# Two-layer hybrid decoder on one core: the experts' low rows subtracted on VectorE instead of GpSimd, with a narrow-product estimate changed and the schedule's priorities drawn anew

## The chip, the cores and the metric

The kernel runs on one core of a Trainium2 chip. The metric is the device time of one execution in microseconds (us), lower is better; the number that counts is the median of three runs. The core's engines appear in the profile as PE (TensorE), DVE (VectorE), ACT (ScalarE), POOL (GpSimd) and SP (SyncE, which issues the transfers from HBM). PEclk is the granted clock of TensorE as a share of its full 2.4 GHz, so 0.50 is the level of 1.2 GHz.

## The reference

T = 256 rows of D = 1024 float32 numbers go through two layers. Each layer adds a mixer, an attention over a memory of its own, and a mixture of 16 experts, each behind an RMS norm:

```
for l in range(DEPTH):
    x = x + hybrid_mixer(rmsnorm(x, mix_norm_g[l]), ...)
    x = x + memory_cross_attention(rmsnorm(x, xattn_norm_g[l]), rmsnorm(mem, mem_norm_g[l]), wq, wkv, wo)
    x = x + hierarchical_moe(rmsnorm(x, ffn_norm_g[l]), wg, bg, we, be, w1, w3, w2)
return rmsnorm(x, final_norm_g)
```

The mixture picks, for each row, one of 4 groups by the largest of 4 logits and two of the group's 4 experts by the largest of their logits; the row then runs through those two experts only, silu(h w1) * (h w3), times w2, weighted.

## The kernel before

**Numbers in two parts.** Products are made at float32 accuracy from TensorE's faster fp32r format. A float32 tensor is rounded to a high part (a copy or activation, mostly on ACT), and the low part is the difference: `split` and `wsplit` put the high part on ACT and the subtraction on DVE. A product is then three matmuls, high by high, high by low and low by high. In the names of the rows `w` is a 1 MB weight buffer, `wh` and `wl` its parts in slices of 512, `mTh` and `mTl` the parts of the memory rows, `yh` and `yl` those of an attention output, `x` the 256 x 1024 stream of rows itself in four blocks of 128 x 512, `ps` a PSUM bank.

**The order.** Nothing runs where it is written. Every call is recorded (line 120 issues them all, so that each row of the profile says L120) and a list scheduler, `Plan.order`, plays the recorded operations through with an estimate of each one's time (`Plan.cost`). On each engine it takes, of what could start now, the operation with the lowest priority number: its place in the program plus a bias for its step and one for its step and engine, from the table `BIAS`. On PE an operation may also be taken that could start up to `LOOK` ns later than the earliest if it has the same form (rows and columns of the array in use, 128 x 128 or a narrower tile), and one of another form is set back by `STICK`. The order that comes out is fixed: every engine runs its list in that order, and waits at an instruction whose inputs are not there.

**The stage around the change.** At the end of the cross attention (steps `wo0` to `wo3`) the blocks of `x` are finished by four adds on DVE (`x<-ps,xsu,x`). Then `route` (steps `r0` and `n0` in the first layer, `r1` and `n1` in the second):

- 16 transposes on PE bring `x` into four PSUM banks (`ps<-cst,x`), and four copies make `qT` of them, three on ACT and one, by `V.tensor_copy if n > b`, on DVE;
- 16 matmuls that fill a quarter of the array each (`ps<-qT,wg`, each two records in the trace) and two small ones (`ps<-cst,t`) give the router's 20 logits `lg`;
- some twenty short DVE operations rank them, down to `asg` and `pos`, and one-hot matrices `S` follow;
- the rows themselves are split for the experts: `nh` is the rounded `x`, two blocks by ACT and two by DVE, and `nl` = `x` - `nh` in four blocks, on GpSimd;
- the experts begin with `ga`, matmuls of `S` by `nh` and by `nl`, which pick each expert's rows (`ps<-S,nh`); then come `up` and `down` for two experts at a time, and `sc`, which puts the results back.

While the router's short chain runs, PE has other work. In layer 0 it is the second layer's memory keys, steps `mk0.1` and `mk1.1`: 48 matmuls of three kinds (`mTh,wh`, `mTl,wh`, `mTh,wl`) into each of two banks, whose `wl` DVE makes slice by slice. In layer 1 nothing is left over, and 24 matmuls whose result is not used (step `idle`, `ps<-nh`) take their place.

Of the kernel before, what the change touches and what calls it, by code (L numbers as in the profile page):

```python
# [13 lines left out]
ALU = mybir.AluOpType  # L14
# [30 lines left out]
HOLD = 0  # L45

DRAIN = 95
STICK = 200
LOOK = 40

LOAD = 0.82
# [72 lines left out]
class Plan:  # L124
# [24 lines left out]
    def cost(self, key, name, args, kw, outs, ins):  # L149
        def free(ap):  # L150
            n = 1
            for s, c in ap.ap[1:]:
                n *= c
            return n

        n = max(free(x) for x in outs[:1] + ins) if ins else free(outs[0])
        if key == "pe":
            w = free(outs[0])
            rhs = args[2] if len(args) > 2 else kw["rhs"]
            if name == "transpose":  # L160
                return max(w * 0.8333, 107) + 2
            if rhs.dtype == F32R:
                c = max(w * (0.4414 if w >= 256 else 1.0) + 5, 109)
            else:
                c = max(w * 1.6667 + 4, 218)
            return c
        psum = any(x.tensor.space == PS for x in ins)
        vec = sum(x.ap[0][1] == P and free(x) == 1 for x in ins[1:])
        if key == "act":
            return n * 0.8333 + (51 if psum else 93) + 93 * vec + 93 * ("accum_out" in kw)  # L170
        if key == "dve":
            if name == "reciprocal":
                return 68 + 6.4 * n
            two = name in ("tensor_tensor", "scalar_tensor_tensor", "tensor_tensor_scan", "tensor_reduce")
            if name == "tensor_tensor_scan":
                return 68 + n * 2.0834
            if not two and not psum:
                return 68 + n * 0.5208 + 61 * (vec > 0)
            return 68 + n * 1.0417 + 61 * (vec > 0)
        return 628 if name == "tensor_tensor" and n < 16 else 150 + 2.1 * n  # L180
# [11 lines left out]
    def note(self, keys, emit, name, args, kw):  # L192
# [24 lines left out]
        op.tiles = []  # L217
        op.prio = op.i + BIAS.get(self.step, 0) + BIAS.get(f"{self.step}/{keys[0]}", 0)
        op.eng, op.wait = keys[0], None
# [42 lines left out]
    def order(self, reserve):  # L262
# [59 lines left out]
        while left:  # L322
            best = None
            for e, cand in ready.items():
# [25 lines left out]
                for s, op in items:  # L350
                    if s <= s_min + (LOOK if e == "pe" and op.form == form else 0):
                        key = op.prio
                        if e == "act" and op.table and table not in op.table:
                            key += 60
                        if e == "pe" and op.form != form:
                            key += STICK
                        if pick is None or key < pick[0]:
# [70 lines left out]
def body(tc, nc, a):  # L428
    def fb(ap):
        return ap.bitcast(F32)  # L430

    with ExitStack() as es:
# [31 lines left out]
        def run(rounds, queue):  # L464
            plan = Plan(tc, nc, queue)
            TE, A, V, G, dq = (plan.queue(k) for k in ("pe", "act", "dve", "pool", "dma"))
# [6 lines left out]
            x = sp.tile([P, 2, D], F32, name="x")  # L473
# [8 lines left out]
            if rounds == 1:  # L482
# [5 lines left out]
                for i in range(4):  # L488
# [4 lines left out]
                    f = slice(i * 512, (i + 1) * 512)  # L493
# [694 lines left out]
            def route(l):  # L1188
# [27 lines left out]
                nh = tp.tile([P, 2, D], F32R, name="nh", tag="th")  # L1216
                nl = tp.tile([P, 2, D], F32R, name="nl", tag="tl")
                for n in range(2):
                    f = slice(n * 512, (n + 1) * 512)
                    for b in range(2):  # L1220
                        plan.step = f"n{l}"
                        (V.tensor_copy if n else A.copy)(nh[:, b, f], x[:, b, f])
                        G.tensor_tensor(nl[:, b, f], x[:, b, f], fb(nh[:, b, f]), op=ALU.subtract)
# [22 lines left out]
                for b in range(2):  # L1246
                    V.tensor_tensor(before[:, b], l5[:, b, :, None, :].to_broadcast([P, 5, 4, 4]), l5[:, b, :, :, None].to_broadcast([P, 5, 4, 4]),
                                    op=ALU.is_ge)
# [39 lines left out]
                w1 = sm.tile([P, 2, 4], F32, name="w1", bufs=1)  # L1288
# [12 lines left out]
                for b in range(2):  # L1301
                    w = pick[:, b * (P + 6 * NPAIR):b * (P + 6 * NPAIR) + 6 * NPAIR].rearrange("p (q c) -> p q c", c=6)
# [190 lines left out]
            for l in range(DEPTH):  # L1493
                mixers(l)
                plan.step = f"x{l}"
                attend(l)
                plan.step = ""
                nxt = l + 1 < DEPTH
                if nxt:
                    memory(l + 1)  # L1500
                plan.step = f"r{l}"
                routed = route(l)
                plan.step = ""
                if nxt:
                    fill(GAP)
                extras = [(kp, "bv"), (kp, "W1"), (kp, "W2"), (sp, "vm")]
                if not nxt:
                    extras += [(sp, "kT"), (sp, "mTh"), (sp, "mTl")]
                extras += [(kp, "qT"), (kp, "xn")] + ["t2"] * (NT2 // 4)
                for rnd in range(rounds):  # L1510
                    end = not nxt and rnd == rounds - 1
                    experts(l, rnd, extras, routed, ending if end else None, last_square if end else None)
# [109 lines left out]
```

## Time and profile before

| | |
|---|---|
| three runs | 731.29, 731.1, 730.45 us; median 731.1 |
| profiled execution | 731.96 us, of which the span from the first to the last instruction is 730.1 |
| busy | PE 712.4 us (98%), DVE 465.8, ACT 355.0, POOL 27.0 |
| mean granted PE clock | 0.992 |
| moved from HBM | 173.19 MB, 239 GB/s over the span |

A busy share says how long an engine had an instruction in flight, not how fast it was: a PE at half its clock is busy too. So the stretches are to be read with the clock beside the busy time, and the small idle time of PE with what released it.

### The profile page before, as it was taken

The numbers are of one execution on the slowest core, as the hardware profiler recorded it, in microseconds if no ns is written. First come the engines' busy times: TensorE is split into PE (matmuls) and PEld (weight loads), VectorE is DVE, ScalarE is ACT, GpSimd is POOL, SyncE is SP. The second block draws the span as 40 slices with busy tenths as digits, with TensorE's granted clock in tenths as the row PEclk, the third lists the DMA queues.
The fourth block names the chain that finished last, engine by engine and source line by source line (L and its number), as shares of the span: only waits on it lengthen the run. The fifth ranks groups of instructions, "written<-read, shape, count | busy, mean of one in ns | idle before, by whom it ended". The sixth has DMA issues, their size and how long they took to land.

```text
span 730.1 us, 12559 instructions
## 1 busy us (share of the span) xinstructions
PE 712.4 (98%) x4864; PEld 559.0 (77%) x4864; DVE 465.8 (64%) x1036; ACT 355.0 (49%) x724; POOL 27.0 (4%) x35
## 2 busy tenths in 40 slices
PE   8999999999999899999999999999999999999995
PEld 8988999989987863554469999888999874544552
DVE  6778699887699741233247669898867893322314
ACT  7666676657566311121146557885656542210212
POOL 0000000100001100000000000001000030000000
PEclk9999999999999899999999999999999999999998
DMA  8832444847645449999864543455577657899911
GB/s 319 334 124 108 140 181 162 308 168 267 213 162 196 174 169 427 401 391 425 331 240 168 181 172 137 145 198 206 174 264 266 234 202 298 350 417 423 386 71 62
DMA packets 30595, 175.13 MB, mean 240 GB/s; under 512 B 3520, under 2 KB 5696, under 8 KB 11072
## 3 DMA queue, kind: packets, MB, share of 16 engines
q1 hardware_dynamic: 30528, 174.25, 62.7%
q8 instruction: 40, 0.66, 0.3%
q14 instruction: 27, 0.22, 0.1%
HBM read 173.19 MB, written 1.05 MB: 239 GB/s over the span
## 4 chain that ended last, share of the span: by engine, by line
PE 88%; DVE 7%; ACT 3%; DMA 1%; issue 1%; SPq 0%; DVEq 0%; POOL 0%; ACTq 0%; POOLq 0%
PE ps L120 88%; DVE wl L120 1%; DVE S L120 1%; DVE OT L120 1%; DMA W<-in_mem 1%; ACT S L120 1%; DVE t L120 1%; DVE x L120 0%; ACT xn L120 0%; DVE nh L120 0%; SPq L120 0%; DVE qT L120 0%; DVE W L120 0%; ACT OT L120 0%; ACT wh L120 0%
## 5 line engine op out<-in xcount | busy, mean ns | idle before, releaser
L120 ACT ACTIVATE wh<-w 128x512 fp32r<-128x512 f32 (+1 forms) x256 | 159.2, 630 | 120.3 <-PE ps L120 110.9
L120 DVE TENSOR_TENSOR wl<-w,wh 128x512 fp32r<-128x512 f32 (+1 forms) x256 | 175.1, 697 | 53.6 <-ACT wh L120 50.3
L120 PE MATMUL ps<-tl,wh 128*128 128x256 f32 x448 | 126.6, 285 | 0.4 <-DVE tl L120 0.4
L120 PE MATMUL ps<-th,wh 128*128 128x256 f32 x448 | 126.4, 284 | 0.0
L120 PE MATMUL ps<-th,wl 128*128 128x256 f32 x448 | 125.6, 284 | 0.2 <-DVE wl L120 0.2
L120 PEld LDWEIGHTS ps<-tl,wh 128*128 128x128 f32 x448 | 84.1, 188 | 1.7 <-issue 1.0
L120 PEld LDWEIGHTS ps<-th,wl 128*128 128x128 f32 x448 | 83.8, 188 | 1.8 <-issue 0.9
L120 PEld LDWEIGHTS ps<-th,wh 128*128 128x128 f32 x448 | 84.2, 188 | 1.1 <-issue 0.5
L120 DVE TENSOR_TENSOR wl<-ps,wh 128x512 fp32r<-128x512 f32 x32 | 21.7, 690 | 65.2 <-ACT wh L120 59.7
L120 DVE SCALAR_TENSOR_TENSOR t<-t,ps 128x256 f32<-128x256 f32 (+1 forms) x20 | 9.5, 474 | 71.2 <-ACT t L120 71.2
L120 PE MATMUL ps<-wl,yh 128*128 128x512 f32 x128 | 50.5, 399 | 0.0
L120 PE MATMUL ps<-wh,yl 128*128 128x512 f32 x128 | 50.0, 397 | 0.0
L120 ACT ACTIVATE wh<-ps 128x512 fp32r<-128x512 f32 x32 | 18.8, 597 | 60.1 <-PE ps L120 60.1
L120 PE MATMUL ps<-wh,yh 128*128 128x512 f32 x128 | 46.2, 397 | 0.0
L120 ACT ACTIVATE t<-ps,cs 128x256 f32<-128x256 f32 x16 | 7.6, 475 | 75.3 <-PE ps L120 72.9
L120 PE MATMUL ps<-mTh,wl 128*128 128x256 f32 x128 | 37.9, 297 | 0.1
L120 PE MATMUL ps<-mTl,wh 128*128 128x256 f32 x128 | 37.2, 291 | 0.0
L120 PE MATMUL ps<-mTh,wh 128*128 128x256 f32 x128 | 37.2, 291 | 0.0
L120 PE MATMUL ps<-wl,mTh 128*128 128x256 f32 x128 | 36.7, 287 | 0.0
L120 PE MATMUL ps<-wh,mTl 128*128 128x256 f32 x128 | 36.2, 283 | 0.0
L120 PE MATMUL ps<-wh,mTh 128*128 128x256 f32 x128 | 36.0, 283 | 0.0
L120 PE MATMUL ps<-S,nh 128*128 128x256 f32 x128 | 32.3, 288 | 0.5 <-DVE pos L120 0.3
(308 smaller groups left out, 1618.7 us busy)
## 6 DMA issues: line engine op xcount, KB each, us to landing
w<-in_ws SPq DMA_DIRECT2D x97, 1024.0 KB, 4.9
W<-in_ws SPq DMA_DIRECT2D x15, 1024.0 KB, 8.2
bv<-in_ws SPq DMA_DIRECT2D x8, 1024.0 KB, 7.6
t<-in_ws SPq DMA_DIRECT2D x28, 256.0 KB, 6.7
vm<-in_ws SPq DMA_DIRECT2D x7, 1024.0 KB, 9.8
qT<-in_ws SPq DMA_DIRECT2D x7, 1024.0 KB, 9.5
xn<-in_ws SPq DMA_DIRECT2D x7, 1024.0 KB, 10.5
mTh<-in_ws SPq DMA_DIRECT2D x3, 1024.0 KB, 9.7
```

Of the source, the lines that this page charges most:

```text
L120: return self.plan.note([self.key], {self.key: lambda: getattr(self.real, name)(*args, **kw)}, name, args, kw)
```

## The change

Three edits. The low part of the experts' rows, `nl`, is subtracted on VectorE (`V.`) where GpSimd (`G.`) did it: eight instructions in all, four in each layer. In `Plan.cost` the estimate of an fp32r matmul loses its case for outputs narrower than 256 (which counted 1.0 ns a column) and its floor goes from 109 to 113 ns. The numbers that set the order, `BIAS`, `STICK` and `LOOK`, are other ones. What is computed, and the number of instructions of every kind, stay as they were.

```diff
-BIAS = {'xs0': 1235, 'cl0': -6235, 'gd0': -710, 'o30': -580, 'm0': 3495, 'w0': 7800,
...
+BIAS = {'xs0': 4070, 'cl0': -850, 'gd0': -450, 'o30': -355, 'm0': -1550, 'w0': 9125,
...
-STICK = 200
-LOOK = 40
+STICK = 300
+LOOK = 20
...
             if rhs.dtype == F32R:
-                c = max(w * (0.4414 if w >= 256 else 1.0) + 5, 109)
+                c = max(w * 0.4414 + 5, 113)
...
                         (V.tensor_copy if n else A.copy)(nh[:, b, f], x[:, b, f])
-                        G.tensor_tensor(nl[:, b, f], x[:, b, f], fb(nh[:, b, f]), op=ALU.subtract)
+                        V.tensor_tensor(nl[:, b, f], x[:, b, f], fb(nh[:, b, f]), op=ALU.subtract)
```

The places where the new order tells are these. On DVE in layer 0's `route`, before: from the last two adds of `x` to the copy `qT` (here `x_90` is the stream, `wl_675` and `wl_677` are slices of the memory key's weight).

```order
L120 SCALAR_TENSOR_TENSOR x_90<-ps_622,xsu_564,x_90 128x512
L120 SCALAR_TENSOR_TENSOR x_90<-ps_623,xsu_564,x_90 128x512
L120 CAST nh_647<-x_90 128x512 x2
L120 TENSOR_TENSOR wl_675<-w_670,wh_674 128x512
L120 TENSOR_TENSOR wl_677<-w_670,wh_676 128x512
L120 COPY qT_632<-ps_634 128x512
```

And the same place after, with the same names (`nl_648` was on POOL before; `w_680` is the next 1 MB of the memory key's weight):

```order
L120 SCALAR_TENSOR_TENSOR x_90<-ps_622,xsu_564,x_90 128x512
L120 SCALAR_TENSOR_TENSOR x_90<-ps_623,xsu_564,x_90 128x512
L120 TENSOR_TENSOR wl_677<-w_670,wh_676 128x512
L120 TENSOR_TENSOR wl_679<-w_670,wh_678 128x512
L120 TENSOR_TENSOR nl_648<-x_90,nh_647 128x512
L120 CAST nh_647<-x_90 128x512 x2
L120 TENSOR_TENSOR nl_648<-x_90,nh_647 128x512 x2
L120 TENSOR_TENSOR wl_683<-w_680,wh_682 128x512
L120 TENSOR_TENSOR wl_685<-w_680,wh_684 128x512
L120 COPY qT_632<-ps_634 128x512
```

Between the last add and `qT` stood two casts and two `wl`; now there are two casts, three `nl` and four `wl`.

On PE at the same place, before: from the last transposes (`ps_636`) over the router's matmuls (`ps_643`, `ps_645`), with the memory key's matmuls (`ps_671`) between.

```order
L120 MATMUL ps_636<-cst_82,x_90 128x128 x4
L120 MATMUL ps_643<-qT_632,wg_631 32x128 x4
L120 MATMUL ps_671<-mTh_625,wh_672 128x256
L120 MATMUL ps_671<-mTl_626,wh_672 128x256
L120 MATMUL ps_671<-mTh_625,wl_673 128x256
L120 MATMUL ps_671<-mTh_625,wh_672 128x256
L120 MATMUL ps_645<-qT_632,wg_631 32x128 x8
L120 MATMUL ps_671<-mTl_626,wh_672 128x256
L120 MATMUL ps_643<-qT_632,wg_631 32x128 x4
```

And after:

```order
L120 MATMUL ps_636<-cst_82,x_90 128x128
L120 MATMUL ps_671<-mTl_626,wh_678 128x256
L120 MATMUL ps_636<-cst_82,x_90 128x128
L120 MATMUL ps_671<-mTh_625,wl_679 128x256
L120 MATMUL ps_671<-mTh_625,wh_678 128x256
L120 MATMUL ps_671<-mTl_626,wh_678 128x256
L120 MATMUL ps_671<-mTh_625,wl_679 128x256
L120 MATMUL ps_643<-qT_632,wg_631 32x128 x4
L120 MATMUL ps_645<-qT_632,wg_631 32x128 x4
L120 MATMUL ps_643<-qT_632,wg_631 32x128 x4
L120 MATMUL ps_645<-qT_632,wg_631 32x128 x4
L120 MATMUL ps_681<-mTh_625,wh_682 128x256
```

The memory key's matmuls now stand between the transposes and ahead of the router's 16 narrow ones, which come without a break; behind the last add of `x` (whose last product is `ps_623`) there are 41 of them before the first `qT,wg`, where there were 5 before the last `qT,wg`.

On DVE in layer 1's `route`, from the third-last add to the second logits, before (`ms2_1387` and `rstd_1388` are the norm's, `rr_1416` its square):

```order
L120 SCALAR_TENSOR_TENSOR x_90<-ps_1377,xsu_1319,x_90 128x512
L120 CAST nh_1395<-x_90 128x512
L120 SCALAR_TENSOR_TENSOR x_90<-ps_1378,xsu_1319,x_90 128x512
L120 CAST nh_1395<-x_90 128x512
L120 COPY qT_1380<-ps_1382 128x512
L120 SCALAR_TENSOR_TENSOR ms2_1387<-ss_1386 128x2
L120 SCALAR_TENSOR_TENSOR lg_1389<-ps_1392,rstd_1388,prm_91 128x20
```

And after:

```order
L120 TENSOR_TENSOR nl_1396<-x_90,nh_1395 128x512
L120 SCALAR_TENSOR_TENSOR x_90<-ps_1377,xsu_1319,x_90 128x512
L120 TENSOR_TENSOR nl_1396<-x_90,nh_1395 128x512
L120 SCALAR_TENSOR_TENSOR x_90<-ps_1378,xsu_1319,x_90 128x512
L120 COPY qT_1380<-ps_1382 128x512
L120 CAST nh_1395<-x_90 128x512
L120 SCALAR_TENSOR_TENSOR ms2_1387<-ss_1386 128x2
L120 CAST nh_1395<-x_90 128x512
L120 TENSOR_TENSOR nl_1396<-x_90,nh_1395 128x512
L120 TENSOR_TENSOR rr_1416<-rstd_1388 128x2
L120 TENSOR_TENSOR nl_1396<-x_90,nh_1395 128x512
L120 SCALAR_TENSOR_TENSOR lg_1389<-ps_1392,rstd_1388,prm_91 128x20
```

The two casts move behind `qT`, and two of the four `nl` stand ahead of it, two behind.

Elsewhere the order differs in many places. Counted over both orders, PE changes the form of its tile 57 times instead of 64. At the start of layer 0's experts PE before ran `ga1.0`, 25 matmuls of `mk1.1` and `ga0.0` (32 matmuls each, of `S` by `nh` and by `nl`) ahead of the first `up`; after, `ga0.0` is followed at once by the `up` matmuls, and `ga1.0` comes later.

## Rows read from the trace of the kernel before

**Rows 1.** The page: the span, and busy time of each engine.

```profile
span 730.1 us, 12559 instructions
PE 712.4 (98%) x4864; PEld 559.0 (77%) x4864; DVE 465.8 (64%) x1036; ACT 355.0 (49%) x724; POOL 27.0 (4%) x35
```

**Rows 2.** Windows: length, busy (PE, PEld, DVE, ACT, POOL), PEclk, DMA share, GB/s.

```profile
234.55:251.55 17.00, 14.69 (x118) 13.15 (x116) 13.49 (x45) 7.43 (x19) 5.31 (x5) 0.80 0.62 241
240.36:247.19 6.83, 6.29 (x34) 5.91 (x35) 3.50 (x16) 1.67 (x4) 0.85 (x2) 0.50 0.62 249
588.50:599.10 10.60, 9.12 (x88) 7.29 (x86) 9.32 (x38) 5.19 (x15) 5.81 (x5) 1.00 0.75 290
720.00:730.10 10.10, 0.97 (x5) 0.44 (x3) 4.65 (x9) 2.45 (x8) 1.63 (x2) 0.75 0.31 112
250.00:270.00 20.00, 19.87 (x142) 15.36 (x142) 12.85 (x55) 5.17 (x11) 0.00 (x0) 1.00 0.29 99
270.00:350.00 80.00, 79.42 (x394) 36.75 (x392) 20.57 (x55) 14.33 (x29) 0.00 (x0) 1.00 1.00 412
```

**Rows 3.** Timeline, layer 0's router, PE: start, duration, instruction, idle before and releaser.

```profile
234.55 0.81 PE L120 MATMUL ps<-cst,x 128*128 128x128 f32 x6
...
240.90 0.65 PE L120 MATMUL ps<-qT,wg 128*32 128x128 f32 x8 [2.10 <-DVE qT L120]
...
249.44 0.37 PE L120 MATMUL ps<-mTh,wh 128*128 128x256 f32 x1
249.65 0.29 PE L120 MATMUL ps<-mTl,wh 128*128 128x256 f32 x1
...
250.12 0.28 PE L120 MATMUL ps<-mTh,wl 128*128 128x256 f32 x1
250.24 0.28 PE L120 MATMUL ps<-mTh,wh 128*128 128x256 f32 x1
```

**Rows 4.** Timeline of the same stretch, DVE.

```profile
234.78 1.40 DVE L120 SCALAR_TENSOR_TENSOR x<-ps,xsu,x 128x512 f32<-128x512 f32 x2
236.10 0.75 DVE L120 CAST nh<-x 128x512 fp32r<-128x512 f32 x2
236.77 3.48 DVE L120 TENSOR_TENSOR wl<-w,wh 128x512 fp32r<-128x512 f32 x2
240.17 0.68 DVE L120 COPY qT<-ps 128x512 f32<-128x512 f32 x1
```

**Rows 5.** Timeline of the same stretch, POOL.

```profile
236.59 3.11 POOL L120 TENSOR_TENSOR nl<-x,nh 128x512 fp32r<-128x512 f32 x2 [0.57 <-DVE nh L120]
```

**Rows 6.** Timeline, DVE, far from any GpSimd work: two `wl` back to back.

```profile
87.40 1.28 DVE L120 TENSOR_TENSOR wl<-w,wh 128x512 fp32r<-128x512 f32 x2
```

**Rows 7.** The tile `nl` over the whole trace: durations in ns, minimum, median, maximum.

```profile
L120 POOL TENSOR_TENSOR nl<-x,nh x8: 1267/1304/1743, 233.0 to 594.5; 128x512 fp32r<-128x512 f32 x8
```

**Rows 8.** Timeline, layer 1's router, DVE and PE.

```profile
587.03 2.27 DVE L120 SCALAR_TENSOR_TENSOR x<-ps,xsu,x 128x512 f32<-128x512 f32 x3
589.33 1.37 DVE L120 CAST nh<-x 128x512 fp32r<-128x512 f32 x1
590.62 0.74 DVE L120 SCALAR_TENSOR_TENSOR x<-ps,xsu,x 128x512 f32<-128x512 f32 x1
591.40 0.96 DVE L120 CAST nh<-x 128x512 fp32r<-128x512 f32 x1
592.28 0.68 DVE L120 COPY qT<-ps 128x512 f32<-128x512 f32 x1
594.88 0.24 DVE L120 SCALAR_TENSOR_TENSOR lg<-ps,rstd,prm 128x20 f32<-128x20 f32 x1 [1.16 <-PE ps L120]
595.04 0.73 DVE L120 TENSOR_TENSOR rr<-rstd 128x2 f32<-128x2 f32 x1
...
599.06 0.35 PE L120 MATMUL ps<-S,nh 128*128 128x256 f32 x1 [0.29 <-DVE pos L120]
```

**Rows 9.** Timeline, DVE: the same `rr` in layer 0, with GpSimd idle.

```profile
254.66 0.15 DVE L120 TENSOR_TENSOR rr<-rstd 128x2 f32<-128x2 f32 x1
```

2 lines of the change are left out of this document (1 added, 1 removed).

## The prediction

> **What bounds the kernel now.** I read the page first. PE is busy for 712.4 of a span of 730.1 us, and DVE, the next, for 465.8 [rows 1]. So nothing can be won but by giving PE less to do, by closing its idle time, which is 730.1 - 712.4 = 17.7 us in all, or by raising its clock where it is low: a PE at half clock counts as busy. The windows show where these lie [rows 2]. Of the idle time 10.10 - 0.97 = 9.1 us is the tail after the last scatter, which this change does not address. In layer 0's router, from the first transpose at 234.55 [rows 3] to the first gather at 251.55, it is 17.00 - 14.69 = 2.3 us, and here alone, away from the tail, the granted clock is low: 0.50, the level of 1.2 GHz, from 240.36 to 247.19, with 6.29 us of PE work in it. In layer 1's router it is 10.60 - 9.12 = 1.5 us, at full clock. What is left, 17.7 - 9.1 - 2.3 - 1.5 = 4.8 us, is spread over the start and many short waits.
>
> Then I followed layer 0's router backward from its one long wait. PE stands for 2.10 us before the `qT,wg` at 240.90, and DVE's `qT` released it [rows 3]. DVE had the last two adds of `x` from 234.78, the casts at 236.10, then two `wl` for 3.48 us, and only at 240.17 the copy `qT` [rows 4]. Two such `wl` in a row take 1.28 us elsewhere [rows 6]. What lies beside the 3.48 us is GpSimd's pair of `nl`, 3.11 us from 236.59 [rows 5]: DVE subtracts nothing while GpSimd does. So 3.48 - 1.28 = 2.2 us of DVE's time, and with it nearly the whole wait, comes from the overlap. The reader is to see the order of events: `nl` starts on POOL, `wl` stretches on DVE, `qT` is late, PE stands, and PE's clock is at half from the end of that wait for 6.8 us.
>
> The same overlap shows in layer 1, smaller: casts of 1.37 and 0.96 us [rows 8] against 0.75 for a pair [rows 4], and a two-column `rr` of 0.73 us [rows 8] against 0.15 where GpSimd is idle [rows 9]. No low clock follows there.
>
> **The change part by part.** *Layer 0's router.* If all its PE work ran at full clock without a wait, the stretch would take 17.00 - 2.31 - 6.29/2 = 11.5 us [rows 2]. How near does the new order come?
>
> First the wait for `qT`. The change puts more in front of `qT` on DVE, not less: by the order, behind the last add of `x` come four `wl`, three `nl` and two casts. A `nl` has the shape and types of a `wl`, so I cost it as one: the pair takes 1.28 us with an overlap of 0.08 between neighbours (the casts begin at 236.10, and the adds before them end at 234.78 + 1.40 = 236.18 [rows 4]), hence 0.60 each in a row. That is 7 x 0.60 + 0.67 = 4.9 us, and `qT` 0.68. The adds end 236.18 - 234.55 = 1.6 us after PE's last product of the attention [rows 3, 4]. So `qT` is there 1.6 + 4.9 + 0.7 = 7.2 us after that product; before it was there 240.85 - 234.55 = 6.3 after. What hides it is PE's work: 41 matmuls of the memory key now stand there ahead of the first `qT,wg`, at 0.12 us each (from 250.12 to 250.24 [rows 3]), 4.9 us, and 14 transposes at about 0.81/6 = 0.12 to 0.135 us, 1.7 to 1.9. That is 6.6 to 6.8 us, so PE still waits 0.4 to 0.6. I take 0.6. Bounds: 0 if the adds start as early as their own bank allows; 1.2 if one `wl` comes late because ACT made its `wh` late. If this cover were not there, PE would stand for longer than before.
>
> *A rule weighed.* The row has the two `wl` at 3.48 us beside `nl`s of 3.11 for two [rows 4, 5]. The Trainium skill (SBUF — State Buffer, "Who interferes with whom") says that a VectorE instruction with two inputs in SBUF and a GpSimd instruction that reads SBUF use one shared pair of ports, held by one at a time for a whole instruction, the later one fully blocked. By that rule the two `wl` would last as long as two `nl` and themselves, 2 x 1.30 + 1.28 = 3.9 us, with the median of `nl` [rows 7]. The trace agrees in kind, 3.48. By the rule the four operations lose 3.9 - 4 x 0.64 = 1.3 us on VectorE when all are put there, by the row 3.48 - 2.56 = 0.9: either way a smaller gain than the 2.2 us of the stall. Neither enters the sum.
>
> Second, the clock. It fell after a stand of 2.1 us; layer 1's waits, 1.5 us in all, were followed by none [rows 2]. With the wait at 0.6 I take the half clock as gone. This is the largest single term, 6.29/2 = 3.15 us, and the least certain.
>
> Third, the chain from the router's matmuls to the first `S`. In layer 1 it takes 599.06 - 592.96 = 6.1 us from the end of `qT` [rows 8], 5.5 without the slow `rr`. In layer 0 DVE has some `wl` between as well, 0.6 each, and PE covers it with 40 matmuls of the second bank of keys, 40 x 0.12 = 4.8 us, and some 2 us of the router's own. I take 0.4 us of idle time left; bounds 0.2 and 1.0.
>
> So the work of that stretch takes 11.5 + 0.6 + 0.4 = 12.5 instead of 17.0: **4.5 us less**. With the bounds: 3.3 to 5.3. (The stretch itself will look longer: of its 118 records [rows 2] 61 were key matmuls, when 16 transposes, 32 records of `qT,wg`, 4 of `cst,t` and 5 of `asg` are taken off, and the new order has 41 + 40 = 81 there. These 20, 2.4 us, are work that stood further on before.)
>
> *Layer 1's router.* PE's filler here has no use, so the chain itself sets the time. On DVE `x` then `nh` then `x` then `nh` then `qT` becomes `nl`, `x`, `nl`, `x`, `qT`. Two casts that took 2.3 us leave, two `nl` of 0.6 come. But three adds already follow one another from 587.03 [rows 8], so the first `nl` delays the third add, and the last add must wait for PE's last product anyway; I get `qT` about 0.4 us earlier, of which the two `nl` and two casts behind it give 0.2 back before the logits (594.88). The `rr` of 0.73, which stood between the logits and the ranking, falls to 0.15: 0.6 more. Together **0.8 us**; bounds 0 (the `nl` behind `qT` hold the logits as long as GpSimd did) and 1.6 (all 1.5 us of idle time there).
>
> *The order elsewhere.* PE changes form 7 times less. A matmul of the key behind a narrow one takes 249.65 - 249.44 = 0.21 us instead of 0.12 [rows 3], so 7 x 0.09 = **0.6 us**; bounds 0 and 1.0. The corrected estimate itself costs nothing on the chip: it acts only through this order. The eight subtractions cost DVE 8 x 0.64 = 5.1 us, which outside the routers nothing waits for, DVE being idle for 730.1 - 465.8 us. GpSimd loses 8 x 1.30 = 10.4 us, which frees nothing but the overlap.
>
> *The experts' start.* Layer 0's first `up` now follows `ga0.0` directly, without the 32 matmuls of `ga1.0` and 25 of the keys ahead of it, (32 + 25) x 0.12 = 6.8 us earlier relative to the gather. Its weights lie there: in 250 to 270 the transfers fill only 0.29 of their share, that is, all buffers are full. From 270 to 350 they run at 1.00, 412 GB/s, and PE idles 0.6 us in 80 [rows 2], so PE and the transfers are nearly balanced. Buffers come free earlier too, which shifts the transfers the same way. I take a loss of **0.3 us**; bounds 0 and one late transfer, 1.05 MB at 412 GB/s or 2.5 us, say 2.0 behind other work.
>
> The sum: 4.5 + 0.8 + 0.6 - 0.3 = 5.6 us. The profiled execution, 731.96, goes to 726.4; it stands 0.9 above the median of the runs, and the median 731.1 goes to **725.5 us**.
>
> **The rivals.** *The clock falls all the same.* The stretch before the low clock held not only the wait but most of the narrow matmuls, and the new order has all of them in a row behind a short wait. If the 3.15 us stay, the gain is 2.4: 728.7 us. For it: the trace cannot separate the two. Against: layer 1 had the same narrow matmuls and a clock of 1.00 [rows 2].
>
> *The wait stays.* DVE's queue ahead of `qT` grows from 4.0 to 4.9 us. If the key's matmuls that should hide it stop, because a `wl` behind a `nl` in the queue is late, PE stands for about 2 us again and the clock falls; layer 1 and the forms give 1.4, the experts take theirs: within 1 us of before, about 730.8. It decides from a stand of some 1.5 us on.
>
> *The rest of the order is better.* Of the 4.8 us of spread idle time half could go, and the terms could reach their upper bounds (5.3 + 1.6 + 1.0): 731.1 - 7.9 - 2.4 = 720.8; typically 721 to 723.
>
> *Slower: weights late in layer 0's experts.* With the `up`s pulled ahead PE runs into transfers that are at 1.00 already. Each 1 MB that is waited for costs 2.5 us; three make 7.6 and end at 725.5 + 7.6 = 733.1. It decides from 5.6 us on. Against it: only the order of PE's work changes, not its amount, and `ga1.0` comes later as cover.
>
> **How the numbers follow.** Chances: the forecast 0.62 (its own range, from the bounds taken together, 724 to 727.5); the clock falls 0.12; the wait stays 0.08; the rest better 0.13; slower 0.05. The range of 721.0 to 729.0 takes in the forecast, the fallen clock and most of the better order, and leaves out the rest, under 2 in 10. A change under about 0.2% (1.5 us) cannot be told from none here. Faster: 0.62 + 0.12 + 0.13 = 0.87; same: 0.08; slower: 0.05.
>
> **What would show it.** Right: POOL has no `nl`; no DVE subtraction in a router lasts over 0.7 us; PE's wait before `qT,wg` in layer 0 is under 1 us; the clock there is 1.00 throughout; from the last attention product to the first `S,nh` it is about 12.5 + 2.4 = 14.9 us in layer 0. In layer 1 `rr` takes 0.15 and the first `S,nh` follows its last attention product sooner by about 0.8. Wrong: a clock of 0.50 in that stretch (the second term fails), waits of PE for `w` or `W` transfers between 250 and 350 (the last term), or a new wait for a low part anywhere else, which the new order alone would have brought.

## The result and the profile after

The changed kernel runs in 721.93 us (median of 4 runs, 720.63 to 722.35), the kernel before in 731.08: a ratio of 0.9873, 95% interval 0.9856 to 0.989, which is 9.2 us or 1.3% less. 725.5 was forecast, so the sign and the range (721.0 to 729.0) held and the gain was 1.6 times the forecast one.

The profiled execution took 720.63 us, the fastest of its four; that of before, 731.96, is the slowest of its own. So the two traces lie 11.3 us apart, 2.2 more than the medians. Numbers from the traces below belong to that larger difference. The trace of before has a stretch of low clock that this kernel does not have in every execution (see fill_wait), so in layer 0's router the traces show more than the medians hold.

The page of after, span and busy time, against [rows 1]:

```profile
span 718.9 us, 12554 instructions
PE 705.9 (98%) x4864; PEld 557.6 (78%) x4864; DVE 463.2 (64%) x1044; ACT 354.1 (49%) x724; POOL 17.8 (2%) x27
```

PE is busy 6.5 us less for the same 4864 records, and idle for 13.0 instead of 17.7 us. The eight `nl` have moved from POOL (35 to 27) to DVE (1036 to 1044).

The windows of after, with the columns of [rows 2]: the two routers, the tail, the stretch between the routers, the one behind the second, and the experts' start of layer 0.

```profile
235.35:248.70 13.35, 13.35 (x137) 13.01 (x136) 12.71 (x51) 7.15 (x16) 0.87 (x2) 1.00 0.89 334
579.89:587.66 7.77, 7.73 (x83) 6.38 (x81) 7.52 (x38) 3.58 (x11) 0.80 (x1) 1.00 0.87 344
708.80:718.80 10.00, 0.39 (x2) 0.00 (x0) 4.29 (x9) 2.04 (x7) 1.51 (x2) 0.64 0.31 111
248.70:579.89 331.19, 331.04 (x2244) 259.66 (x2243) 210.03 (x439) 161.91 (x324) 7.09 (x7) 1.00 0.65 251
587.66:708.80 121.14, 120.56 (x640) 60.72 (x640) 37.45 (x122) 24.52 (x52) 0.00 (x0) 1.00 0.72 296
250.00:270.00 20.00, 20.00 (x116) 10.48 (x115) 7.26 (x39) 3.29 (x8) 0.00 (x0) 1.00 0.67 267
270.00:350.00 80.00, 79.93 (x405) 38.63 (x406) 23.45 (x65) 15.94 (x33) 0.00 (x0) 1.00 0.97 392
```

And two windows of before that were not shown yet, the same two stretches, from its first `S,nh` of layer 0 to the end of layer 1's last attention product, and from `S,nh` of layer 1 to the tail:

```profile
251.55:589.50 337.95, 336.62 (x2273) 261.09 (x2272) 212.61 (x442) 162.36 (x324) 6.27 (x8) 1.00 0.65 247
599.06:720.00 120.94, 120.35 (x637) 61.12 (x638) 37.29 (x120) 24.77 (x51) 0.00 (x0) 1.00 0.72 294
```

Both routers now run with PE busy from end to end, and at a clock of 1.00. Taken apart by these windows:

| stretch | before | after | difference | key matmuls moved in or out |
|---|---|---|---|---|
| to the last attention product of layer 0 | 234.55 | 235.35 | +0.8 | 9 records more, +1.1 |
| router of layer 0, to the first `S,nh` | 17.00 | 13.35 | -3.65 | 20 more, +2.4 |
| from there to the last attention product of layer 1 | 337.95 | 331.19 | -6.76 | 29 fewer, -3.4 |
| router of layer 1 | 9.56 | 7.77 | -1.8 | |
| the rest | 131.0 | 131.2 | +0.2 | |

(Moved records at 0.118 us each, the spacing of the key matmuls. In before layer 1's router is 589.50 to 599.06.) With the moved work taken off, layer 0's router gave 3.65 + 2.4 = 6.0 us, layer 1's 1.8, and the stretch between them 3.3, of which 1.2 is idle time of PE (1.33 to 0.15).

DVE in layer 0's router of after, the answer to [rows 4]:

```profile
235.28 1.40 DVE L120 SCALAR_TENSOR_TENSOR x<-ps,xsu,x 128x512 f32<-128x512 f32 x2
236.60 1.28 DVE L120 TENSOR_TENSOR wl<-w,wh 128x512 fp32r<-128x512 f32 x2
237.80 0.68 DVE L120 TENSOR_TENSOR nl<-x,nh 128x512 fp32r<-128x512 f32 x1
238.40 0.75 DVE L120 CAST nh<-x 128x512 fp32r<-128x512 f32 x2
239.07 1.28 DVE L120 TENSOR_TENSOR nl<-x,nh 128x512 fp32r<-128x512 f32 x2
240.28 1.28 DVE L120 TENSOR_TENSOR wl<-w,wh 128x512 fp32r<-128x512 f32 x2
241.48 0.68 DVE L120 COPY qT<-ps 128x512 f32<-128x512 f32 x1
```

And PE at its end, the answer to [rows 3]:

```profile
241.65 0.28 PE L120 MATMUL ps<-mTh,wl 128*128 128x256 f32 x1
241.85 1.08 PE L120 MATMUL ps<-qT,wg 128*32 128x128 f32 x32
242.87 0.39 PE L120 MATMUL ps<-mTh,wh 128*128 128x256 f32 x1
```

No wait is printed. The copy begins 241.48 - 235.35 = 6.1 us behind PE's last attention product, later than before (240.17 - 234.55 = 5.6), and ends at 242.16, when PE is still in the first half of its 32 narrow records, which do not read this copy. So `qT` is not earlier; what has changed is what PE does meanwhile.

DVE in layer 1's router of after, the answer to [rows 8]:

```profile
579.17 0.75 DVE L120 SCALAR_TENSOR_TENSOR x<-ps,xsu,x 128x512 f32<-128x512 f32 x1
579.84 0.68 DVE L120 TENSOR_TENSOR nl<-x,nh 128x512 fp32r<-128x512 f32 x1
580.44 0.74 DVE L120 SCALAR_TENSOR_TENSOR x<-ps,xsu,x 128x512 f32<-128x512 f32 x1
581.10 0.68 DVE L120 COPY qT<-ps 128x512 f32<-128x512 f32 x1
...
583.10 0.16 DVE L120 TENSOR_TENSOR rr<-rstd 128x2 f32<-128x2 f32 x1
...
584.04 0.24 DVE L120 SCALAR_TENSOR_TENSOR lg<-ps,rstd,prm 128x20 f32<-128x20 f32 x1 [0.18 <-PE ps L120]
```

From the last attention product (589.50 before, 579.89 after) `qT` begins after 1.21 us instead of 2.78, the logits after 4.15 instead of 5.38, and `rr` is back to 0.16.

### The profile page after: what moved, and what is told of

The parts are those of the page before. It is cut to its first block, busy times and chain, and to the rows that moved or that the text cites. A ratio compares the mean times of both kernels' runs of the same rounds, so it can differ in the third digit from the quotient of the medians.

```text
span 718.9 us, 12554 instructions
## 1 busy us (share of the span) xinstructions
PE 705.9 (98%) x4864; PEld 557.6 (78%) x4864; DVE 463.2 (64%) x1044; ACT 354.1 (49%) x724; POOL 17.8 (2%) x27
## 4 chain that ended last, share of the span: by engine, by line
PE 91%; ACT 3%; DMA 2%; DVE 2%; issue 1%; SPq 0%; DVEq 0%; ACTq 0%
PE ps L120 91%; DMA w<-in_ws 2%; DMA W<-in_mem 1%; ACT S L120 1%; DVE OT L120 0%; DVE wl L120 0%; DVE t L120 0%; SPq L120 0%; ACT OT L120 0%; ACT t L120 0%; ACT wh L120 0%; ACT yh L120 0%; ACT jk L120 0%; ACT L424 0%; ACT L120 0%
## 5 line engine op out<-in xcount | busy, mean ns | idle before, releaser
L120 DVE TENSOR_TENSOR wl<-w,wh 128x512 fp32r<-128x512 f32 (+1 forms) x256 | 172.8, 687 | 51.4 <-ACT wh L120 45.7
L120 PE MATMUL ps<-tl,wh 128*128 128x256 f32 x448 | 124.3, 281 | 0.0
L120 ACT ACTIVATE t<-ps 128x512 fp32r<-128x512 f32 (+2 forms) x42 | 21.2, 514 | 26.9 <-PE ps L120 26.8
```

What stands on the lines that cost most here:

```text
L120: return self.plan.note([self.key], {self.key: lambda: getattr(self.real, name)(*args, **kw)}, name, args, kw)
```

## The experiments

The theory at this point: the move to VectorE removes a collision, but in layer 0 it is the new order, with the key matmuls laid ahead of the router's products, that takes away PE's wait, and with the wait goes the low clock (theory A). The rival (theory B): the collision, DVE's subtractions held up by GpSimd's, is the whole cause, and the order adds little. To part them the scheduler's order was kept fixed. A list of the recorded operations in the order of before or of after takes the scheduler's place, and it says which of the eight `nl` run on GpSimd:

```diff
+    def kept(self):
+        out, table = [self.ops[i] for i in ORDER], "ln"
+        for op in out:
+            op.eng = "pool" if op.i in ON_POOL else op.engines[0]
...
-            plan.issue(plan.order(RESERVE) if rounds == 1 else plan.ops)
+            plan.issue(plan.kept() if rounds == 1 else plan.ops)
```

Each time is compared with runs of the kernel before on the same chip; that kernel's median there was 730.6 to 732.0.

**move_only: the engine without the order.** `ORDER` is that of before, `ON_POOL` is empty.

> The order of before kept on every engine; only the eight nl instructions run on DVE, at the places that the order gives them. Theory A (the overlap with GpSimd made only part of the wait; the new order did the rest): in layer 0 DVE now has x, nl, x, two casts, nl, wl, wl, nl ahead of qT, so qT comes at about 239.9 instead of 240.2, PE still stands for some 1.8 us, and the clock falls to 0.50 for over 6 us as before. Layer 1 gains 0.8 (no stretched casts) and 0.6 (rr at 0.15). Time 731.1 - 0.3 - 1.4 = 729.4 us. Theory B (the overlap is the whole cause): the stand in layer 0 goes, the clock stays at 1.00, the time is 724 to 726 us.

729.08 us, ratio 0.9981 (0.9966 to 0.9996), 1.4 us less. One row of its PE timeline, and its windows of layer 0's router, of the low clock in it, and of layer 1's router:

```profile
240.94 0.43 PE L120 MATMUL ps<-qT,wg 128*32 128x128 f32 x8 [1.11 <-DVE qT L120]
```

```profile
234.84:250.32 15.48, 13.64 (x117) 12.07 (x116) 13.14 (x48) 7.53 (x19) 0.85 (x2) 0.89 0.67 264
242.52:245.93 3.41, 3.41 (x17) 3.41 (x17) 2.40 (x13) 1.20 (x2) 0.00 (x0) 0.50 0.86 332
588.30:596.86 8.56, 7.75 (x83) 6.45 (x81) 7.86 (x40) 4.20 (x13) 1.07 (x1) 1.00 0.84 319
```

No subtraction collides any more, and in this trace PE still idles for 1.84 us in layer 0 and is granted 0.50 for 3.41 us. Layer 0 gives 1.5 us, layer 1 gives 1.0, and the time stays 7 us above that of after. The rival falls. (The low clock is not the rule in this kernel: the traced execution, 730.48 us, is one of two in twelve with a mean clock below 0.995; see fill_wait.)

**nl_back: the order without the engine.** `ORDER` is that of after, `ON_POOL` holds all eight `nl`.

> The order of after kept on every engine; only the eight nl run on GpSimd again. Theory A (order first): in layer 0 the two wl ahead of qT are stretched to about 3.4 us by the nl beside them, but two nl leave DVE's queue, so qT comes 0.5 us later at most; PE's 41 key matmuls cover that, no stand over 1 us, clock 1.00. In layer 1 the casts and rr are stretched as before and about 1.3 us are lost. Time 721.9 + 1.5 = 723.4 us. Theory B (the overlap is the whole cause): PE stands for about 2 us in layer 0, the clock falls, the time is 727 us or more.

723.12 us, ratio 0.9904 (0.9881 to 0.9928). DVE and POOL around `qT`, then the windows of the two routers:

```profile
240.25 3.49 DVE L120 TENSOR_TENSOR wl<-w,wh 128x512 fp32r<-128x512 f32 x2
243.67 0.68 DVE L120 COPY qT<-ps 128x512 f32<-128x512 f32 x1
```

```profile
240.07 3.12 POOL L1232 TENSOR_TENSOR nl<-x,nh 128x512 fp32r<-128x512 f32 x2 [3.48 <-DVE nh L120]
```

```profile
236.52:250.88 14.36, 13.89 (x137) 13.10 (x136) 13.73 (x48) 7.22 (x17) 4.06 (x5) 1.00 0.85 311
581.85:590.62 8.77, 7.99 (x83) 6.50 (x81) 7.83 (x35) 3.55 (x11) 4.11 (x4) 1.00 0.90 346
```

The collision is back in full, 3.49 us for two `wl` as in [rows 4], and costs 1.0 us in each router (14.36 against 13.35, 8.77 against 7.77): PE idles for 0.47 us in layer 0, and the clock stays. So in layer 0's traces the order gave 5.0 of the 6.0 us and the engine 1.0 (1.5 in the order of before, by move_only); in layer 1 the engine gave 1.0 of 1.8, in either order.

**fill_wait: is it the stand that lowers the clock?** (A stand is the time in which PE has nothing to do but wait.) Before, with PE's wait filled:

```diff
+                if self.extra and op.i == EXTRA_AT:
+                    for _ in range(EXTRA_N):
+                        self.extra()
                 op.emit[op.eng]()
...
+                        plan.extra = lambda o=o: nc.tensor.matmul(o[:, 256:512], nh[:, 1, 0:128], nh[:, 1, 256:512], start=True, stop=True)
```

> Before, unchanged in order and engines, with 18 more matmuls (128x256, of nh, results not used) put on PE right ahead of the qT,wg that waits in layer 0, 2.1 us of work in a stand of 2.10 us. Theory A (the stand lowers the clock): no low clock in layer 0, the 3.15 us of half clock are saved, time 731.1 - 3.1 = 728.0 us. Rival (the narrow matmuls of the router lower it): the clock is 0.50 there as before, time 731 us.

730.14 us, ratio 0.9987 (0.9968 to 1.0005). Its PE timeline and window:

```profile
239.46 2.31 PE L1225 MATMUL ps<-nh 128*128 128x256 f32 x18
```

```profile
235.38:249.69 14.31, 14.11 (x135) 12.79 (x134) 13.10 (x45) 7.53 (x19) 5.32 (x5) 1.00 0.59 239
```

The clock stays at 1.00 with the same narrow matmuls, and the stretch takes 14.31 instead of 17.00 us. But the time of the whole kernel shows 0.5 us of the 2.7, and its interval ends at 2.3; the profiled execution's span, 728.4 against 730.1, keeps 1.7 of it, its layer 0 router having begun 0.8 us later.

Where the rest went, the mean granted clock of each execution shows. It is 0.992 to 0.994 in the five traces of this document with a low clock ahead of the tail (before, move_only, late_qT, h_rest, old_stick) and 0.995 to 0.997 in the eight without one. Of the 23 executions of before that stand beside fill_wait, 12 have 0.994 or less and a median of 732.1 us, and 11 have 0.995 or more and 729.5. All twelve of fill_wait have 0.995 or more. So before loses its clock in only a part of its executions (here 12 of 23, on the chips of the later experiments 29 of 39), at some 2.6 us each time, and its median mixes the two kinds. The mean takes in the tail as well, so for a single execution it is a sign and not a proof; but with the stand filled not one in twelve shows it.

**late_qT: the stand put into after.** The same hook, with `nc.vector.tensor_tensor(nl[:, 1, 512:1024], ...)` four times ahead of `qT`, and `ORDER` that of after.

> After, unchanged in order and engines, with the last block of nl subtracted four more times on DVE right ahead of the copy qT in layer 0, 4 x 0.60 = 2.4 us. Theory A: PE stands about 2 us before the qT,wg that needs this copy, the clock falls to 0.50 for 6 to 7 us behind it, and the price is the stand and the half clock, 2.1 + 3.1: time 727.1 us. Rival (the low clock of before had another cause, such as the many narrow matmuls or the weak stretch ahead of the stand): the clock stays at 1.00 and the price is the stand alone, 724.0 us.

725.83 us, ratio 0.993 (0.9904 to 0.9956), about 4 us over after. Its PE timeline, with the 32 narrow records in two halves, and windows:

```profile
242.68 0.64 PE L120 MATMUL ps<-qT,wg 128*32 128x128 f32 x16
245.84 1.08 PE L120 MATMUL ps<-qT,wg 128*32 128x128 f32 x16 [2.52 <-DVE qT L120]
```

```profile
236.17:255.13 18.96, 16.44 (x137) 15.62 (x136) 15.94 (x56) 7.40 (x17) 0.87 (x2) 0.82 0.71 256
245.47:252.30 6.83, 6.46 (x41) 6.05 (x42) 4.60 (x21) 1.16 (x3) 0.87 (x2) 0.50 0.45 156
```

A stand of 2.52 us, with it 6.83 us at 0.50, and the stretch is 18.96 - 13.35 = 5.6 us longer: the stand and half of 6.46. Five of the six executions have a mean clock of 0.992 to 0.994 and take 725.3 to 727.0 us; the sixth has 0.996 and takes 722.77. So a stand of this length brings the low clock in most executions, not in all, and filling the stand keeps it away.

**Hybrids: where the rest of the gain lies.** `ORDER` is that of after up to a point and that of before behind it, or the reverse, each list without what the first part has issued. In short (the kernels hold the finished list):

```diff
-ORDER = pos["before"]
+first = pos["after"][:cut]
+ORDER = first + [i for i in pos["before"] if i not in first]
```

> The instructions that the order of after issues up to its first S,nh of layer 0 stand in the order of after (nl of layer 0 on DVE); all others follow in the order of before (nl of layer 1 on GpSimd). Theory A (layer 0's router is the bulk; in the profiles it gives 6.0 us once the 20 key matmuls that moved into it are taken off): 731.1 - 6.0 = 725.1 us, low clock gone. Rival (the gain lies spread over the new order): 728 us or more.

727.85 us, ratio 0.9952 (0.9935 to 0.997).

> The complement: the order of before up to its first S,nh of layer 0 (nl of layer 0 on GpSimd), then all others in the order of after (nl of layer 1 on DVE). Theory A: the low clock of layer 0 stays, layer 1's router gives 1.8, the order elsewhere 1.3: 731.1 - 3.1 = 728.0 us. Rival (spread gain as the profiled executions have it, 5.2 us outside layer 0's router): 726 us.

726.92 us, ratio 0.9941 (0.9918 to 0.9964). Windows of h_router0 (its router, then the stretch at the seam), and of h_rest (its router, then up to the last attention product of layer 1):

```profile
236.20:250.34 14.14, 13.52 (x137) 13.01 (x136) 13.50 (x53) 7.36 (x17) 0.87 (x2) 1.00 0.90 338
250.00:260.00 10.00, 8.64 (x70) 8.47 (x71) 7.84 (x36) 1.90 (x4) 0.00 (x0) 1.00 0.14 58
```

```profile
234.79:255.34 20.55, 18.25 (x147) 16.71 (x145) 15.51 (x51) 8.18 (x21) 5.29 (x5) 0.83 0.50 202
255.34:586.43 331.09, 330.93 (x2245) 259.77 (x2244) 209.35 (x437) 161.64 (x324) 7.11 (x7) 1.00 0.66 252
```

The low clock is gone from the one and there in the other, as expected, but the sizes are not those of theory A: 3.5 us instead of 6.0, and 4.3 instead of 3.1. The 6.0 had taken the low clock of one trace for that of every execution of before; on this chip 14 of 18 have it. And there is a cost of the seam, where one order passes into the other (PE idles 1.4 us in 250 to 260). In h_rest the router's 20.55 us hold 29 records more than in before, key matmuls worth 3.4 us, and the stretch between the routers, 331.09 us, is that of after. So the order there is worth its 3 us without layer 0's router.

> The order of after up to the last attention product of layer 1, then the order of before with nl of layer 1 on GpSimd. Theory A: only layer 1's router is given back, 1.8 us: 721.9 + 1.8 = 723.7 us. Rival (the order of layer 1's experts and of the last transfers matters as well): 725 us or more.

722.25 us, ratio 0.9878 (0.9859 to 0.9898). Its window of layer 1's router:

```profile
580.21:589.07 8.86, 7.85 (x82) 6.52 (x81) 7.66 (x37) 3.56 (x11) 4.53 (x4) 1.00 0.86 341
```

Theory A's 1.8 us are not in the time. In the trace the router gives back 1.1 (8.86 against 7.77), and the rest, 719.6 - 589.1 = 130.5 us, is 0.7 shorter than in after. In sum the order of layer 1's end matters by less than the runs can tell.

**replan: the move alone, planned anew.** Before with `V.tensor_tensor` for `nl`, as in the change's last hunk, and nothing else.

> Before with nl on VectorE and nothing else: the old table, estimate, STICK and LOOK, and the scheduler free to place the subtractions. By its order, 18 key matmuls stand between the transposes and the qT,wg that waits, and from the last add to qT there are three wl, two nl and one cast. Theory A: a stand of about 0.7 us, clock 1.00, 4.5 us from layer 0 and 1 to 1.4 from layer 1: 725.5 us. Rival (without the new table the move gives what it gave in the old order): 729 us.

730.21 us, ratio 0.9981 (0.997 to 0.9992). Its windows of the two routers and between:

```profile
235.29:249.31 14.02, 13.39 (x128) 11.82 (x126) 13.51 (x50) 8.20 (x20) 0.81 (x2) 1.00 0.75 296
249.31:588.48 339.17, 338.06 (x2263) 260.33 (x2262) 212.27 (x440) 162.08 (x324) 5.91 (x7) 1.00 0.65 246
588.48:597.41 8.93, 7.81 (x83) 6.43 (x81) 8.09 (x42) 4.02 (x13) 0.69 (x1) 1.00 0.74 275
```

Layer 0's router gives 3.0 us, 4.2 with the 10 key matmuls that came in, and the clock is 1.00. But the stretch between the routers grew by 1.2 us with these 10 gone, so by 2.4 in truth: one changed line moves the order behind it too. PE changes form 34 times there instead of 28 (by the records of the trace), which at about 0.2 us each, the price worked out below, makes up to 1.2 of the 2.4, by estimate. The rival's number was right, for another reason than it named: the gain was made and given back.

**old_cost and old_stick: the other two edits.** After with `c = max(w * (0.4414 if w >= 256 else 1.0) + 5, 109)`; and after with `STICK = 200`, `LOOK = 40`.

> After with the old estimate for narrow products, all else (nl on VectorE, table, STICK, LOOK) as in after. The order on DVE around qT in layer 0 is that of after. Theory A: the estimate counts only through the order, both routers run as in after, a few places elsewhere change: 721.9 to 723 us. Rival (the estimate carries a good part of the gain outside the routers): 724 us or more.

722.05 us, ratio 0.9867 (0.9845 to 0.989): the same as after. The corrected estimate by itself brings nothing that can be measured.

> After with STICK = 200 and LOOK = 40, all else as in after. The order differs in many places: the last add of x in layer 0 comes later, behind 44 key matmuls. Theory A (these two numbers are what keeps PE's changes of form few, which gave about 1.6 us between the routers): 723.5 us, with more changes of form. Rival (the table alone decides): 722 us.

729.6 us, ratio 0.9976 (0.9959 to 0.9994), over 7 us more than after. PE's timeline and a window, in the mixer of layer 1, and the window between the routers:

```profile
487.47 0.58 PE L120 MATMUL ps<-wl,mTh 128*128 128x256 f32 x1 [1.54 <-DVE wl L120]
```

```profile
487.33:490.75 3.42, 3.28 (x15) 3.28 (x16) 1.45 (x4) 0.47 (x1) 1.98 (x3) 0.50 0.98 402
249.51:587.07 337.56, 335.62 (x2250) 260.00 (x2249) 210.23 (x440) 161.65 (x324) 5.63 (x7) 0.99 0.65 247
```

Neither theory had this time: the table belongs to its `STICK` and `LOOK`, and with others a `wl` is late 240 us further on, PE stands for 1.54 us, and a low clock comes with it. Theory A had a part of it right: PE changes form 30 times between the routers instead of 22. That stretch is 6.4 us longer than in after, of which 1.8 are idle time, 1.6 half clock (half of 3.28), 0.5 four more key matmuls, and by estimate up to 1.6 changes of form; some 0.9 or more is not assigned.

**h_to_s1: a better mix?**

> The order of after up to its first S,nh of layer 1 (all nl on DVE), then the order of before for layer 1's experts. In the profiles the stretch from that S,nh to the end took 131.2 us in after and 130.5 in the kernel that ends in the order of before from layer 1's router on. Theory A (that difference belongs to the experts' order): 721.9 - 0.7 = 721.2 us, a little faster than after. Rival (it is scatter between executions, or the seam costs as much): 721.9 us or more.

720.73 us, ratio 0.9847 (0.9834 to 0.9861). The window behind its first `S,nh` of layer 1:

```profile
588.43:710.24 121.81, 121.22 (x640) 59.53 (x639) 38.00 (x120) 25.58 (x53) 0.00 (x0) 1.00 0.73 295
```

That is no shorter than the 121.14 of after, so theory A falls, and the intervals of the two ratios overlap. It is not shown to be faster.

## Why the prediction was right in sign and small in size

- *The collision* was read rightly: `nl` on DVE takes 0.68 us, no subtraction in a router lasts over 0.69, and nl_back brings the 3.49 us back. By the sentence weighed there from the Trainium skill (SBUF — State Buffer, "Who interferes with whom"), two `wl` beside two `nl` would last 3.9 us; 3.48 and 3.49 were measured, so it holds in kind, and its size is a little high. Its worth in layer 0 is about the 0.9 that the row gave (1.0 in nl_back, 1.5 in move_only). The other sentence, that nearly the whole wait comes from the overlap, does not hold for the move: without any collision 1.84 of 2.31 us of idle time stayed (move_only).
- *DVE's queue ahead of `qT`*, forecast at 4.9 us from the adds' end, took 241.48 - 236.60 = 4.9. PE's cover, forecast at 6.6 to 6.8 us from the last product, took 241.85 - 235.35 = 6.5.
- *The wait left before `qT,wg`*, the term of 0.6 us, was mis-sized: it is 0, its lower bound. The adds ended 1.3 us behind the last product (235.28 + 1.40 - 235.35), not 1.6, which is the case that the lower bound named, so `qT` was there after 6.8 us instead of 7.2. That alone would leave 0.3; the rest is a mistake in what waits. The copy on DVE fills one of four banks, and in the new order half of the narrow records, 16, which read others, stand ahead of the first that reads it (late_qT shows its wait between the halves) and take the 0.5 us that cover it. *The chain to `S`*, 0.4, was 0 as well, below its bound of 0.2. With both at 0 the router would give 5.5; it gave 6.0, and the other 0.5 is not assigned.
- *The clock*, 3.15 us, held in the traces: 1.00 throughout after, and a mean of 0.995 or 0.996 in all four of its executions. fill_wait and late_qT show that it hangs on the stand, not on the narrow matmuls. But the sum took before's trace for the usual execution. By the mean clock 41 of 62 executions of before in the experiments lost it, at some 2.6 us each, which makes 1.7 us in the mean (an estimate; for the result's own runs of before the clock is not recorded).
- *Layer 1's router*, 0.8 us, gave 1.8, above its bound of 1.6. The step that failed is `qT` "about 0.4 us earlier": I let the last add wait for PE's last product, but what held it was DVE's queue: it began 1.1 us behind that product before, after the cast of 1.37 us, and 0.55 behind it now. And `qT`, whose bank holds other blocks than that add's, waited in the queue for the cast of 0.96 us, which the new order puts behind it: 1.0 more. So it came 1.6 us earlier.
- *The order elsewhere*, 0.6 us, and the experts' start, -0.3, together gave 3.3 in the profiles. The rival "the rest of the order is better" had the place right. PE's idle time between the routers fell by 1.2 us, which the sum had at nothing; the experts' start lost nothing (PE 20.00 of 20 and 79.93 of 80 us, transfers at 0.67 and 0.97). The remaining 2.1 us are records that follow one another more closely. Changes of form are part of it: counted over the records, 28 became 22 in that stretch, and one costs more than the 0.09 us that I took from the narrow tiles. On the way out of the experts' 64-column products in after:

```profile
301.93 2.31 PE L120 MATMUL ps<-W,t 128*64 128x512 f32 x10
304.18 0.50 PE L120 MATMUL ps<-wl,OT 128*128 128x512 f32 x1
304.51 0.39 PE L120 MATMUL ps<-wh,OT 128*128 128x512 f32 x1
304.74 0.39 PE L120 MATMUL ps<-wl,OT 128*128 128x512 f32 x1
```

The first full-width product takes 304.51 - 304.18 = 0.33 us instead of 0.23, and the ten narrow ones 2.25 us where pairs 0.43 apart elsewhere make 2.15: 0.2 in all. Six of these would be 1.2 us, which is an upper figure, since three of the six are changes into the narrow form, whose price is not worked out here; the last 0.9 or more is not assigned.

In the medians the gain is 9.2, not 11.3. How it divides among the parts is known only in the traces, and the hybrids' 3.5 and 4.3 us sum to 7.8. The time of 721.93 lies outside the forecast's own range of 724 to 727.5 and within the 721 to 723 of the rival "the rest of the order is better", which had a chance of 0.13. Two errors went opposite ways: without the clock the sum was 2.45 us, where some 7.5 are left of the 9.2 by the estimate above, and the clock was worth less than 3.15. With all of its 3.15 the time would have come near 720.5, below the range, so that the range held is in part luck.

## What to carry to other kernels

When a slow neighbour on a shared path makes an engine late, look first at what the waiting engine could do meanwhile: in layer 0's traces the new order gave 4.5 to 5.0 us and removing the collision 1.0 to 1.5. A stand of TensorE is to be priced with the low clock that can come with it, which in the trace of before cost more than the stand (3.15 against 2.10 us); but not every execution has it, so look at the clock of many executions before a trace's price is put into a sum. And where a list scheduler decides, a one-line move is a new order everywhere: compare orders with the one held fixed, or the gain of the line and the luck of the order are not told apart.

## What the runs showed of the hardware

- With a stand of 2.10 us and of 2.52 us (before, late_qT) the granted clock was 0.50 for 6.83 us, from 0.5 and 0.4 us before the stand's end; where the stands were 0.34, 0.39 and 1.11 us within 5.3 us (move_only), and with one of 1.54 us (old_stick), it was 0.50 for 3.41 and 3.42. In layer 1's router of before, 1.5 us of idle time in pieces were followed by none.
- The same program does not lose the clock in every execution. By the mean clock (0.994 or less) it fell in 41 of 62 executions of before, 5 of 6 of late_qT, 2 of 12 of move_only, 9 of 9 of old_stick, and in none of the 12 of fill_wait.
- Two VectorE subtractions beside two GpSimd ones took 3.48 and 3.49 us in two different orders, against 1.28 alone.
